# A causal depthwise convolution shared anew between TensorE, VectorE, ScalarE and GpSimd

## The chip, the cores and the metric

The kernel runs on one core of a Trainium2 chip. Its time is the device time of one execution, in microseconds (us). The engines are PE (TensorE, matrix products), DVE (VectorE), ACT (ScalarE), POOL (GpSimd) and SP (SyncE, which issues the DMAs). Each runs its own list of instructions in order and waits for the others through semaphores. SBUF is the working memory of 128 partitions; PSUM holds what PE writes, in eight banks of 128 x 512 float32. POOL works on SBUF only.

## The reference

A trunk of two layers on 256 tokens of width 2048, all in float32. Layer 0 mixes tokens with a convolution module, layer 1 with latent attention; a squared-ReLU MLP follows each. The change touches the convolution module alone:

```python
def conv_module(h, w_pw1, b_pw1, w_dw, b_dw, ln_g, ln_b, w_pw2, b_pw2):
    u = h @ w_pw1 + b_pw1
    a, gate = jnp.split(u, 2, axis=-1)
    u = a * jax.nn.sigmoid(gate)
    u = lax.conv_general_dilated(
        u, w_dw[:, None, :].astype(u.dtype), window_strides=(1,),
        padding=[(CONV_WIDTH - 1, 0)],
        dimension_numbers=("NWC", "WIO", "NWC"),
        feature_group_count=D_MODEL) + b_dw
    u = jax.nn.silu(layer_norm(u, ln_g, ln_b))
    return u @ w_pw2 + b_pw2
```

## The kernel before

Weights come from memory as float32. Each tile of them is split into a rounded part "hi" (by ACT, line 154) and a remainder "lo" (by DVE or POOL, line 155), and a product is made of three fast matmuls: hi with hi, hi with lo, lo with hi. Inputs of the first product, xh and xl, are split the same way once, at the start.

The convolution stage works channel by channel: 16 chunks (KC) of 128 channels, channels on the partitions, 256 tokens along the row. The loop over c from 1 to 16 is software-pipelined by hand, under `tc.manual_schedule()`, so that each engine executes its instructions in the order in which the program writes them. Turn c does the first product of chunk c (`conv_mm`, 96 matmuls, lines 485 to 487, into two PSUM tiles `pss[c]`: values and gates), and the rest of chunk c-1:

- `glu(c-1)`: ACT takes the sigmoid of the gates (line 502), DVE multiplies it with the biased values (line 503). The result `ub` has 30 zeros ahead of it, which POOL writes (line 499). It has three buffers.
- `pe_taps(c-1)`: PE does the first taps. A tap is a product with a diagonal 128 x 128 matrix of its weights (`diag`, made by ACT, line 509), on a window of `ub`. It is a float32 product, which PE runs in two passes (line 518). Chunk 0 has none, chunks 1 to 13 have 3, chunk 14 has 6, chunk 15 has 19. ACT then adds the bias into the same PSUM tile (line 521).
- `dve_taps(c-1)`: DVE does the remaining taps, each one scalar_tensor_tensor (weight times window plus sum, line 552), on a sum in PSUM. It alternates between chunk c-2 and chunk c-1. At the end of a turn 16 taps of chunk c-1 are left over (REST), and a turn begins with four taps of the older chunk (LEAD). Two PSUM banks hold the sums.
- `to_tokens(c-3)`: PE transposes a finished chunk back to tokens (line 579); DVE takes statistics for the layer norm (`ln_stats`, line 589) and ACT copies the tile (line 591).
- `conv_half`: the splits of weight units, four halves in a turn, with lo on POOL.
- From turn 2 on, eight adds on POOL (line 692) put the second product's bias into the residual `xs`.

After the loop come the last chunk's tail (some filler transposes, `keep_warm`, line 220; the last sums, lines 545 and 548), the layer norm (lines 704 to 717), the swish (lines 720 to 737), and the second product with its own loop over m. The chunk's taps, in the order given by these lines, end the stage.

Of the kernel before, what the change touches and what calls it, by code (L numbers as in the profile page):

```python
# [10 lines left out]
F32 = mybir.dt.float32  # L11
# [3 lines left out]
AF = mybir.ActivationFunctionType  # L15
ALU = mybir.AluOpType
AX = mybir.AxisListType

P = 128
D = 2048  # L20
KC = D // P
T = 2
S = T * P
FF = 4 * D
NB = 512
NNB = D // NB
W = 31
PAD = W - 1
# [12 lines left out]
PAD_O = 56  # L41
WB = 6
LOOK = WB // 2 - 1
PE_TAPS = (3, 3, 3, 3)
PE_MORE = (3, 16)
LEAD = 4
REST = (16, 12)
N_WARM = 14
N_WARM_LN = (8, 26, 14)
EPS = 1e-6  # L50
# [22 lines left out]
def trunk_kernel(  # L73
# [26 lines left out]
    nc = tc.nc  # L100
# [8 lines left out]
    def repool(name, **banks):  # L109

        psum_cx[0].close()
        psum_cx[0] = ExitStack()
        for kind, n in banks.items():
            psum[kind] = psum_cx[0].enter_context(tc.tile_pool(name=kind + name, bufs=n, space=PSUM, reuse_waits="tile"))
# [13 lines left out]
    def nm(s):  # L128
        uid[0] += 1
        return f"{s}_{uid[0]}"  # L130


    def acc_tile():
        return psum["acc"].tile([P, NB], F32, tag="acc", name=nm("acc"))

    def tr_tile():
        return psum["tr"].tile([P, NB], F32, tag="tr", name=nm("tr"))
# [107 lines left out]
        for j in range(2):  # L245
            lo_part(ps[j], hi(k0 + j), lo(k0 + j), gain[:, k0 + j : k0 + j + 1])

    repool("c", acc=4, tr=2, sum=2)


    xs = main.tile([P, T, D], F32, name="xs")
# [181 lines left out]
    with ExitStack() as cx:  # L433
# [32 lines left out]
        def conv_half(n, h):  # L466
            if n < NU + KC // 2:
                wjs[n, h] = split_half(raws[n], h, nc.gpsimd if 0 < n + h and n < NU + 2 else nc.vector)
# [17 lines left out]
                    nc.tensor.matmul(o, wh[:, bs], xl(k), start=False, stop=False)  # L486
                    nc.tensor.matmul(o, wl[:, bs], xh(k), start=False, stop=k == KC - 1)  # L487

        pss, ubs, pcs, cas, cts = {}, {}, {}, {}, {}
        n_pe = lambda c: 0 if c == 0 else PE_TAPS[c % 4] + {KC - 2: PE_MORE[0], KC - 1: PE_MORE[1]}.get(c, 0)  # L490
        rest = lambda c: {KC - 2: REST[1], KC - 1: 0}.get(c, REST[0])
        tap = lambda c, w: w_dw[:, w * KC + c : w * KC + c + 1]

        def sum_tile():
            return psum["sum"].tile([P, NB], F32, tag="sum", name=nm("sum"))

        def glu(c):
            ub = ubs[c] = cv2.tile([P, PAD + S], F32, tag="ub", name=nm("ub"), bufs=3)
            nc.gpsimd.memset(ub[:, 0:PAD], 0.0)
            sg = cv2.tile([P, S], F32, tag="sg", name=nm("sg"))  # L500
            va, ga = pss.pop(c)
            nc.scalar.activation(sg, ga[:, :S], AF.Sigmoid, bias=b_pw1[:, KC + c : KC + c + 1])
            nc.vector.scalar_tensor_tensor(
                out=ub[:, PAD:], in0=va[:, :S], scalar=b_pw1[:, c : c + 1], in1=sg, op0=ALU.add, op1=ALU.mult
            )

        def diag(c, w):
            dg = cv2.tile([P, P], F32, tag="dg", name=nm("dg"), bufs=16)
            nc.scalar.activation(dg, ident, AF.Copy, scale=tap(c, w))
            return dg  # L510

        def pe_taps(c, dgs):

            pc = pcs[c] = sum_tile()[:, :S]
            for w in range(n_pe(c)):
                if w == len(dgs):
                    dgs.append(diag(c, w))
                nc.tensor.matmul(pc, dgs[w], ubs[c][:, w : w + S], start=w == 0, stop=w == n_pe(c) - 1)  # L518
            left[c] = list(range(n_pe(c), W))
            if 0 < c < KC - 1:  # L520
                nc.scalar.activation(pc, pc, AF.Identity, bias=b_dw[:, c : c + 1])  # L521
            elif c:

                pcs[c], last_sum[:] = acc_tile()[:, :S], [pc]

        left, last_sum = {}, []

        def ca_part(c):
            if c // 2 not in cas:
                cas[c // 2] = cv2.tile([P, 2, S], F32, tag="ca", name=nm("ca"))  # L530
            return cas[c // 2][:, c % 2, :]

        def dve_tap(c):
            w = left[c].pop(0)
            out = pcs[c]
            if c in (0, KC - 1) and w == n_pe(c):
                nc.vector.tensor_scalar(
                    out, ubs[c][:, w : w + S], scalar1=tap(c, w), scalar2=b_dw[:, c : c + 1],
                    op0=ALU.mult, op1=ALU.add,
                )  # L540
                return
            if c == KC - 1:
                if not left[c]:
                    half = cv2.tile([P, S], F32, tag="half", name=nm("half"), bufs=1)
                    nc.vector.scalar_tensor_tensor(
                        out=half, in0=ubs[c][:, w : w + S], scalar=tap(c, w), in1=out, op0=ALU.mult, op1=ALU.add
                    )
                    nc.vector.tensor_tensor(ca_part(c), last_sum[0], half, op=ALU.add)
                    return
            elif not left[c]:  # L550
                out = ca_part(c)
            nc.vector.scalar_tensor_tensor(  # L552
                out=out, in0=ubs[c][:, w : w + S], scalar=tap(c, w), in1=pcs[c], op0=ALU.mult, op1=ALU.add
            )

        def dve_taps(c, rest, fill):


            n = 0
            while len(left[c]) > rest or left.get(c - 1):  # L560
                if left.get(c - 1):
                    dve_tap(c - 1)
                if n < LEAD and c < KC - 1 and left.get(c - 1):
                    if fill:
                        fill.pop(0)()
                elif len(left[c]) > rest:
                    dve_tap(c)
                n += 1
            while fill:
                fill.pop(0)()  # L570

        def to_tokens(c):

            if c % 2 == 0:
                cts[c // 2] = tr_tile()
            ct = cts[c // 2]
            for t in range(T):
                q = 2 * t + c % 2
                nc.tensor.transpose(
                    ct[:, q * P : (q + 1) * P], cas[c // 2][:, c % 2, t * P : (t + 1) * P], ident  # L580
                )

        def ln_stats(c):
# [22 lines left out]
        with tc.manual_schedule():  # L606
# [27 lines left out]

            def turn0(n):
                for j in range(2):
                    pt = acc_tile() if n == 2 else sum_tile() if n == 1 else None
                    to_T(xn, 4 * n + 2 * j, xh, xl, g_mix[0], pt)


# [18 lines left out]
                turn(w_dw[:, i * NW : (i + 1) * NW], w_rows[i])  # L659
            conv_split(2)  # L660
            conv_mm(0, 12)
            dgs = []
            fills = []
            for c in range(1, KC + 1):
                n = UC * c
                conv_load(n + 3)
                glu(c - 1)
                fills += ln_stats(c - 4) if c > 3 else []
                fill, fills = fills[: 1 + c % 2], fills[1 + c % 2 :]
                if c < KC:  # L670
                    pss[c] = [acc_tile() for _ in range(2)]
                    conv_mm(c, 0, 2)
                conv_half(n + 1, 0)
                pe_taps(c - 1, dgs)
                conv_half(n + 1, 1)
                dve_taps(c - 1, rest(c - 1), fill)
                conv_load(n + 4)
                if c < KC:
                    conv_mm(c, 2, 6)
                    conv_half(n + 2, 0)  # L680
                    conv_half(n + 2, 1)
                    conv_mm(c, 8)
                    dgs = [diag(c, w) for w in range(min(n_pe(c), 16))]
                if c > 2:
                    to_tokens(c - 3)
                if c < KC:
                    conv_mm(c, 12)
                if 2 <= c < 2 + T * NNB:

                    t, i = divmod(c - 2, NNB)  # L690
                    sl = slice(i * NB, (i + 1) * NB)
                    nc.gpsimd.tensor_tensor(xs[:, t, sl], xs[:, t, sl], b2[:, sl], op=ALU.add)
            warm(AF.Sqrt)
            keep_warm(ident, N_WARM_LN[0])
            to_tokens(KC - 2)
            for f in fills + ln_stats(KC - 3):
                f()
            to_tokens(KC - 1)
            for f in ln_stats(KC - 1):
# [47 lines left out]
            for m in range(NP):  # L747
                if m + 3 < NP:
                    ln_norm(m + 3)
                if m + 2 < NP:  # L750
                    ln_swish(m + 2)
                for j in range(2):
                    k = 2 * m + j
                    wh, wl = conv_w(NU + m, j)
                    for b in range(2):
                        bs = slice(b * NB, (b + 1) * NB)
                        for t in range(T):
                            mm3(ps2[b][t], sh_kt(k, t), sl_kt(k, t), wh[:, bs], wl[:, bs], k == 0, k == KC - 1)
                conv_split(NU + m + 2)
                conv_load(NU + m + 5)  # L760

        ssq, add, prepare = residual_stage(True, g_mlp[0])
        for b in range(2):
# [590 lines left out]
```

## Time and profile before

| | |
|---|---|
| time, median of 3 runs | 2014.34 us (2014.23 to 2014.4) |
| the profiled execution | 2014.3 us, span 2012.4 us |
| granted TensorE clock over the span | 0.998 |
| convolution stage | from about 31 us (first sigmoid) to 234.06 us (aggregate of the layer norm's statistics) |

In the profile, a row of a group gives line, engine, operation, output and inputs, shapes, the count, busy time and mean duration in ns, and the idle time ahead of it with what ended it. A row of the timeline begins with its start and duration in us; "x3" means that three neighbours of one kind are merged, and a bracket gives the idle time ahead and its releaser. Instructions of one engine overlap in part: the distance between two starts can be less than a duration.

### The profile page before, as it was taken

To read this page: it belongs to the slowest core of one execution; us is meant where nothing else is said; L and a number is where in the kernel's file an instruction comes from. 1 tells how busy PE (TensorE), PEld (TensorE's weight loads), DVE (VectorE), ACT (ScalarE), POOL (GpSimd) and SP (SyncE) were. 2 spreads that over 40 slices of the span, in tenths; PEclk is the share of its full clock that TensorE was granted. 3 is DMA by queue.
4 is the path that set the end of the run, shared out by engine and by line. 5 is a ranking of instruction groups with operands and counts; after the bars stand their busy time and mean duration, and the time that the engine had idled before them with its cause. 6 is when DMAs were issued, how large, how long until landed. Compare 5 with 4: busy or idle time off the path is not lost.

```text
span 2012.4 us, 28002 instructions
## 1 busy us (share of the span) xinstructions
PE 1989.3 (99%) x11144; PEld 1743.9 (87%) x11144; DVE 1217.5 (61%) x1806; ACT 966.0 (48%) x1372; POOL 209.3 (10%) x156
## 2 busy tenths in 40 slices
PE   7999999999999999999999999999999999999998
PEld 7999888888888888888889998888888888888886
DVE  6999866665554466555546675665654545565453
ACT  5444665544434354444446665544543334454443
POOL 5887300000000000000000510000000000000000
PEclk9999999999999999999999999999999999999999
DMA  7555355666555666555545445666655556665553
GB/s 237 168 168 168 126 188 179 198 189 188 189 197 199 189 189 188 189 192 192 192 144 186 131 146 171 206 190 188 189 192 198 197 188 188 189 189 194 199 192 105
DMA packets 243266, 367.58 MB, mean 183 GB/s; under 512 B 15416, under 2 KB 89792, under 8 KB 242880
## 3 DMA queue, kind: packets, MB, share of 16 engines
q1 hardware_dynamic: 242400, 364.68, 56.9%
q8 instruction: 87, 1.43, 0.3%
q10 hardware_dynamic: 736, 1.12, 0.2%
q14 instruction: 43, 0.35, 0.0%
HBM read 363.68 MB, written 2.10 MB: 182 GB/s over the span
## 4 chain that ended last, share of the span: by engine, by line
PE 96%; DVE 2%; ACT 1%; DMA 0%; issue 0%; POOL 0%; SPq 0%; ACTq 0%; DVEq 0%
PE acc L399 23%; PE acc L182 16%; PE acc L180 16%; PE acc L181 16%; PE acc L400 12%; PE acc L486 3%; PE acc L485 3%; PE acc L487 3%; PE sum L518 1%; PE tr L237 1%; DMA xs<-in_x 0%; PE acc L1128 0%; PE acc L992 0%; PE acc L994 0%; PE acc L993 0%
## 5 line engine op out<-in xcount | busy, mean ns | idle before, releaser
L155 DVE TENSOR_TENSOR lo<-raw,hi 128x1024 fp32r<-128x1024 f32 (+2 forms) x629 | 759.7, 1211 | 694.8 <-ACT hi L154 682.9
L154 ACT ACTIVATE hi<-raw 128x1024 fp32r<-128x1024 f32 (+1 forms) x696 | 723.6, 1046 | 787.3 <-PE acc L181 451.2
L399 PE MATMUL acc<-xt,hi 128*128 128x512 f32 x2048 | 710.6, 390 | 0.0
L400 PE MATMUL acc<-xt,lo 128*128 128x256 f32 x2048 | 577.7, 282 | 0.0
L399 PEld LDWEIGHTS acc<-xt,hi 128*128 128x128 f32 x2048 | 384.4, 188 | 80.5
L180 PE MATMUL acc<-hi,gh 128*128 128x512 f32 x1024 | 398.6, 389 | 0.0
L182 PE MATMUL acc<-lo,gh 128*128 128x512 f32 x1024 | 398.4, 389 | 0.0
L181 PE MATMUL acc<-hi,gl 128*128 128x512 f32 x1024 | 398.4, 389 | 0.0
L400 PEld LDWEIGHTS acc<-xt,lo 128*128 128x128 f32 x2048 | 387.1, 189 | 0.1
L182 PEld LDWEIGHTS acc<-lo,gh 128*128 128x128 f32 x1024 | 192.2, 188 | 39.9
L180 PEld LDWEIGHTS acc<-hi,gh 128*128 128x128 f32 x1024 | 192.2, 188 | 39.8
L181 PEld LDWEIGHTS acc<-hi,gl 128*128 128x128 f32 x1024 | 192.2, 188 | 39.7
L552 DVE SCALAR_TENSOR_TENSOR sum<-ub,w_dw,sum 128x256 f32<-128x256 f32 x404 | 168.5, 483 | 2.8 <-ACT sum L521 0.7
L155 POOL TENSOR_TENSOR lo<-raw,hi 128x1024 fp32r<-128x1024 f32 x67 | 159.3, 2400 | 56.6 <-ACT hi L154 56.6
L485 PE MATMUL acc<-xt,hi 128*128 128x256 f32 x512 | 147.0, 287 | 0.0
L486 PE MATMUL acc<-xt,hi 128*128 128x256 f32 x512 | 143.2, 280 | 1.0 <-DVE xt L193 1.0
L487 PE MATMUL acc<-xt,lo 128*128 128x256 f32 x512 | 143.0, 279 | 0.0
L486 PEld LDWEIGHTS acc<-xt,hi 128*128 128x128 f32 x512 | 96.3, 188 | 1.6 <-DVE xt L193 1.2
L485 PEld LDWEIGHTS acc<-xt,hi 128*128 128x128 f32 x512 | 96.3, 188 | 0.4
L487 PEld LDWEIGHTS acc<-xt,lo 128*128 128x128 f32 x512 | 96.2, 188 | 0.0
L923 POOL MEMSET pad_kv<- 128x8 f32 x1 | 0.1, 105 | 772.6 <-PE acc L182 772.6
L407 ACT ACTIVATE v<-acc 128x256 f32<-128x256 f32 x128 | 46.3, 381 | 25.4 <-PE acc L400 25.4
(230 smaller groups left out, 1787.1 us busy)
## 6 DMA issues: line engine op xcount, KB each, us to landing
raw<-in_mlp_w SPq DMA_DIRECT2D x256, 1024.0 KB, 5.1
raw<-in_conv_w_pw SPq DMA_DIRECT2D x64, 512.0 KB, 5.1
raw<-in_conv_w_pw SPq DMA_DIRECT2D x16, 1024.0 KB, 4.9
raw<-in_mla_w_o SPq DMA_DIRECT2D x16, 1024.0 KB, 5.2
raw<-in_mla_w_kv_up SPq DMA_DIRECT2D x8, 1024.0 KB, 5.4
raw<-in_mla_w_in SPq DMA_DIRECT2D x8, 576.0 KB, 3.7
raw<-in_mla_w_in SPq DMA_DIRECT2D x4, 1024.0 KB, 6.5
raw<-in_mla_w_q_up SPq DMA_DIRECT2D x16, 256.0 KB, 3.6
```

Of the source, the lines that this page charges most:

```text
L154: nc.scalar.activation(hi, raw[:, js, :], AF.Copy)
L155: eng.tensor_tensor(lo, raw[:, js, :], hi.bitcast(F32), op=ALU.subtract)
L180: nc.tensor.matmul(ps, sh, mh, start=start, stop=False)
L181: nc.tensor.matmul(ps, sl, mh, start=False, stop=False)
L182: nc.tensor.matmul(ps, sh, ml, start=False, stop=stop)
L399: nc.tensor.matmul(ps[b], wh[:, bs], xhl(k), start=k == 0, stop=False)
L400: nc.tensor.matmul(ps[b][:, :S], wl[:, bs], xh(k), start=False, stop=k == KC - 1)
L407: nc.scalar.activation(v[:, b, :], o[:, S:], AF.Copy)
L485: nc.tensor.matmul(o, wh[:, bs], xh(k), start=k == 0, stop=False)
L486: nc.tensor.matmul(o, wh[:, bs], xl(k), start=False, stop=False)
L487: nc.tensor.matmul(o, wl[:, bs], xh(k), start=False, stop=k == KC - 1)
L552: nc.vector.scalar_tensor_tensor(out=out, in0=ubs[c][:, w : w + S], scalar=tap(c, w), in1=pcs[c], op0=ALU.mult, op1=ALU.add)
```

## The change

- PE's taps go, but for the last chunk, which has 22 (LAST_PE). Its 22 diagonals are made by ACT over turns 13 to 15.
- For every other chunk, the first tap is done by ACT, bias included, into the PSUM sum (`start_sum`). The next two taps (five in chunk 14, four in chunk 15) are products made by ACT in SBUF (`product`), added to each other by POOL (`side_sum`) and joined to the sum by one DVE add, written as a `None` at position 14 in the chunk's list of taps.
- Gating: ACT copies the values with their bias to SBUF, and POOL multiplies them with the sigmoid. The last chunk is gated by DVE as before.
- DVE's order: a loop takes entries of the two oldest unfinished chunks in turn. The newest chunk begins after 7 entries (LEAD), and a turn ends when 16, 18 and from then on 22 entries of all chunks are left.
- Sums have three PSUM banks, transposes one; some transposes of the start and of the last pair of chunks use other tiles.
- `conv_half(n + 1, 0)` comes ahead of the first product's matmuls, which are no longer cut around the taps.
- The bias adds on `xs` move into the second product's loop.

```diff
-PE_TAPS = (3, 3, 3, 3)
-PE_MORE = (3, 16)
-LEAD = 4
-REST = (16, 12)
+LAST_PE = 22
+SIDE = 2
+LAST_SIDE = (5, 4)
+JOIN = 14
+LEAD = 7
+REST = (16, 18, 22)
...
-    repool("c", acc=4, tr=2, sum=2)
+    repool("c", acc=4, tr=1, sum=3)
...
-            nc.vector.scalar_tensor_tensor(
-                out=ub[:, PAD:], in0=va[:, :S], scalar=b_pw1[:, c : c + 1], in1=sg, op0=ALU.add, op1=ALU.mult
-            )
+            if c == KC - 1:
+
+                nc.vector.scalar_tensor_tensor(
+                    out=ub[:, PAD:], in0=va[:, :S], scalar=b_pw1[:, c : c + 1], in1=sg, op0=ALU.add, op1=ALU.mult
+                )
+            else:
+                vb = cv2.tile([P, S], F32, tag="vb", name=nm("vb"))
+                nc.scalar.activation(vb, va[:, :S], AF.Identity, bias=b_pw1[:, c : c + 1])
+                nc.gpsimd.tensor_tensor(ub[:, PAD:], vb, sg, op=ALU.mult)
+
+        def product(c, w):
+            pr = cv2.tile([P, S], F32, tag="tp", name=nm("tp"), bufs=sum(LAST_SIDE) + SIDE)
+            nc.scalar.activation(pr, ubs[c][:, w : w + S], AF.Copy, scale=tap(c, w))
+            return pr
...
+        def start_sum(c):
+            w = 0
+            if c < KC - 1:
+                pcs[c] = sum_tile()[:, :S]
+                nc.scalar.activation(
+                    pcs[c], ubs[c][:, 0:S], AF.Identity, bias=b_dw[:, c : c + 1], scale=tap(c, 0)
+                )
+                w = 1
+            else:
+                pcs[c] = acc_tile()[:, :S]
+                o = sum_tile()[:, :S]
+                last_sum.append(o)
+                for w in range(LAST_PE):
+                    nc.tensor.matmul(o, dgs[w], ubs[c][:, w : w + S], start=w == 0, stop=w == LAST_PE - 1)
+                w = LAST_PE
+            n = n_side(c)
+            sides[c] = [product(c, w + i) for i in range(n)]
+            left[c] = list(range(w + n, W))
+            left[c].insert(min(JOIN, len(left[c]) - 1), None)
+
+        def side_sum(c):
+            ps = sides[c]
+            step = 1
+            while step < len(ps):
+                for i in range(0, len(ps) - step, 2 * step):
+                    nc.gpsimd.tensor_tensor(ps[i], ps[i], ps[i + step], op=ALU.add)
+                step *= 2
...
         def dve_tap(c):
             w = left[c].pop(0)
             out = pcs[c]
-            if c in (0, KC - 1) and w == n_pe(c):
+            if w is None:
+                nc.vector.tensor_tensor(out, out, sides[c][0], op=ALU.add)
+                return
+            if c == KC - 1 and w == LAST_PE + n_side(c):
...
+        def dve_taps(c, fill):
+
+
+            n, last = 0, turns.get("last")
+            lead = 0 if c in (0, KC - 1) else LEAD
+            while sum(len(v) for v in left.values()) > rest(c):
+                ready = [k for k in sorted(left) if left[k] and (k < c or n >= lead)]
+                if not ready:
+                    break
+                k = next((k for k in ready[:2] if k != last), None)
+                if fill and (k is None or n >= LEAD - 2):
+                    fill.pop(0)()
+                if k is None:
+                    k = ready[0]
+                dve_tap(k)
+                last = turns["last"] = k
                 n += 1
...
-                cts[c // 2] = tr_tile()
+                cts[c // 2] = acc_tile() if c == KC - 2 else tr_tile()
...
-                fills += ln_stats(c - 4) if c > 3 else []
-                fill, fills = fills[: 1 + c % 2], fills[1 + c % 2 :]
+                fill = ln_stats(c - 4) if c > 3 else []
+                fill, copies = fill[:T], fill[T:]
                 if c < KC:
                     pss[c] = [acc_tile() for _ in range(2)]
-                    conv_mm(c, 0, 2)
-                conv_half(n + 1, 0)
-                pe_taps(c - 1, dgs)
+                    conv_half(n + 1, 0)
+                start_sum(c - 1)
+                if c == KC:
+                    side_sum(c - 1)
+                    conv_half(n + 1, 0)
                 conv_half(n + 1, 1)
-                dve_taps(c - 1, rest(c - 1), fill)
+                dve_taps(c - 1, fill)
                 conv_load(n + 4)
                 if c < KC:
-                    conv_mm(c, 2, 6)
+                    side_sum(c - 1)
+                    conv_mm(c, 0, 8)
                     conv_half(n + 2, 0)
                     conv_half(n + 2, 1)
+                    for f in copies:
+                        f()
                     conv_mm(c, 8)
-                    dgs = [diag(c, w) for w in range(min(n_pe(c), 16))]
+                    if c > KC - 4:
+                        dgs.extend(diag(KC - 1, w) for w in range(len(dgs), min(len(dgs) + 8, LAST_PE)))
                 if c > 2:
                     to_tokens(c - 3)
                 if c < KC:
                     conv_mm(c, 12)
-                if 2 <= c < 2 + T * NNB:
-
-                    t, i = divmod(c - 2, NNB)
-                    sl = slice(i * NB, (i + 1) * NB)
-                    nc.gpsimd.tensor_tensor(xs[:, t, sl], xs[:, t, sl], b2[:, sl], op=ALU.add)
...
                 conv_split(NU + m + 2)
                 conv_load(NU + m + 5)
+
+                t, i = divmod(m, NNB)
+                sl = slice(i * NB, (i + 1) * NB)
+                nc.gpsimd.tensor_tensor(xs[:, t, sl], xs[:, t, sl], b2[:, sl], op=ALU.add)
```

## What the time should do: prediction before the run

> **What bounds the kernel now.** The page first: one engine is busy from end to end, and the rows of 40 slices show GpSimd at work in the first six only, which is the convolution stage that the change edits.
>
> ```profile
> span 2012.4 us, 28002 instructions
> PE 1989.3 (99%) x11144; PEld 1743.9 (87%) x11144; DVE 1217.5 (61%) x1806; ACT 966.0 (48%) x1372; POOL 209.3 (10%) x156
> POOL 5887300000000000000000510000000000000000
> 125.00:150.00 25.00, 25.00 (x206) 24.68 (x205) 23.68 (x60) 11.23 (x20) 21.16 (x13) 1.00 0.58 170
> ```
>
> The last row is from the table of stretches (PE, PEld, DVE, ACT, POOL busy, then clock, DMA). The averages over the span mislead: within the stage DVE is 95% busy and POOL 85%, at full clock. I read next the chain of waits there, and the waits of the stage (who for whom: total, times, longest).
>
> ```profile
> 107.16 1.31 PE sum L518 x6
> 119.90 1.31 PE sum L518 x6
> 209.16 2.61 PE sum L518 x12
> ACT sg L502 <- PE acc L487: 85.5, 16, 6.1
> ```
>
> The chain is TensorE's all through: one chunk per 12.74 us (119.90 - 107.16), in which the six passes of three diagonal taps take 1.31. ACT and DVE wait for PE. So PE sets the turn, and DVE stands 5% behind it.
>
> **PE.** Gone are the taps of chunks 1 to 14, 13 x 3 + 6 = 45; a tap is 1.31 / 3 = 0.437. The turn falls to 12.74 - 1.31 = 11.43. The gate inputs give the times:
>
> ```profile
> 31.13 0.47 ACT L502 ACTIVATE sg<-acc,vecs 128x256 f32<-128x256 f32 x1 [4.97 <-PE acc L487]
> 42.33 0.47 ACT L502 ACTIVATE sg<-acc,vecs 128x256 f32<-128x256 f32 x1 [6.06 <-PE acc L487]
> 221.84 0.47 ACT L502 ACTIVATE sg<-acc,vecs 128x256 f32<-128x256 f32 x1 [2.02 <-PE acc L487]
> 27.12 0.38 PE L276 MATMUL tr<-ident,stage 124*128 124x124 f32 x2
> 27.77 0.52 PE L276 MATMUL tr<-ident,stage 124*128 124x124 f32 x2 [0.27 <-DVE w_dw L277]
> ```
>
> A turn without taps and transposes takes 42.33 - 31.13 = 11.20. The transpose pool drops from two banks to one, so the four transposes of the tap weights wait for DVE's copy three times instead of once. One such step is 27.77 - 27.12 = 0.65, against some 0.13 between two that needn't wait (0.38 for a pair): 2 x 0.52 = 1.0 later. Sigmoids then start at 32.1 (chunk 0), 43.3, 54.5, 65.9 (chunk 3), and by PE alone at 65.9 + 12 x 11.43 = 203.1 for chunk 15. It starts at 221.84 today.
>
> **DVE.** It loses the gating STT; a chunk's first tap goes to ACT and two to ACT plus POOL, in place of three on PE, and one add joins them. A turn before: 28 taps, one gating, one bn_stats on average. After: 28 taps, one join, the same bn_stats. The count is equal; only the order differs. Prices:
>
> ```profile
> 227.98 0.39 DVE acc L552
> 228.38 0.39 DVE sum L552
> 32.81 7.32 DVE L552 SCALAR_TENSOR_TENSOR sum<-ub,w_dw,sum 128x256 f32<-128x256 f32 x14
> 107.10 0.42 DVE L589 BATCH_NORM_STATS2 stats<-tr 128x6 f32<-128x256 f32 x1
> 107.44 0.47 DVE L552 SCALAR_TENSOR_TENSOR sum<-ub,w_dw,sum 128x256 f32<-128x256 f32 x1
> 232.39 0.42 DVE L548 TENSOR_TENSOR ca<-sum,half 128x256 f32<-128x256 f32 x1
> ```
>
> Taps that alternate between two sums cost 0.39 each; taps in a row on one sum (14 of chunk 0) cost (7.32 - 0.48) / 13 = 0.53. bn_stats holds DVE for 0.34, and I give the join the same: its nearest row is the add L548 (0.42 long, sources in PSUM and SBUF). Playing the new loop through by hand (7 entries of older chunks, then the two oldest in turn, 22 left over), from turn 5 on no two neighbours share a sum, where today four or two per turn do. An even turn is 28 x 0.39 + 0.34 = 11.3, one with two bn_stats 12.0, mean 11.65. That is above PE's 11.43, so DVE becomes the bound, narrowly. Turn 4 still waits for chunk 3: sigmoid at 65.9, plus bias copy, gating and first tap, 2.25 (below); 22 taps more end at 76.8. Ten turns of 11.65 give 193.3, and turn 15 (27 taps, a join, two bn_stats: 11.6) 204.9. The gating of chunk 15, which stays on DVE, starts there.
>
> **ACT and POOL.** The edits that I cost at nothing are covered as follows.
>
> ```profile
> L502 ACT ACTIVATE sg<-acc,vecs 128x256 f32<-128x256 f32 x16 | 7.6, 476 | 85.5 <-PE acc L487 85.5
> L521 ACT ACTIVATE sum<-sum,vecs 128x256 f32<-128x256 f32 x14 | 6.3, 448 | 19.3 <-PE sum L518 19.3
> L509 ACT ACTIVATE dg<-ident,w_dw 128x128 f32<-128x128 f32 x64 | 20.5, 393 | 0.5 <-PE sum L518 0.4
> L155 POOL TENSOR_TENSOR lo<-raw,hi 128x1024 fp32r<-128x1024 f32 x67 | 159.3, 2400 | 56.6 <-ACT hi L154 56.6
> 110.01 7.12 POOL L155 TENSOR_TENSOR lo<-raw,hi 128x1024 fp32r<-128x1024 f32 x3 [0.32 <-ACT hi L154]
> L692 POOL TENSOR_TENSOR xs<-xs,b 128x512 f32<-128x512 f32 x8 | 10.4, 1302 | 0.0
> L1050 POOL TENSOR_TENSOR qhl<-qp,qhl 128x256 fp32r<-128x256 f32 x8 | 5.9, 746 | 4.1 <-ACT qhl L186 4.1
> ```
>
> ACT drops three diagonals (0.39 each) and gains a bias copy (at most 0.48) and two products (about 0.42); the first tap replaces L521. ACT is 45% busy, so only its order counts. In turns 13 to 15 it adds 22 diagonals, behind all it owes to others. POOL trades one 1.30 add for a gating and a side sum: 128x256 costs 0.75 in another stage (L1050). A turn is four halves at (7.12 - 0.05) / 3 = 2.36, 9.44, plus 1.5, plus a memset of 0.13: 11.05. The gating now waits for ACT, with four splits queued behind it on POOL and the first tap, products and second hi behind it on ACT. From the start of the sigmoid: bias copy to 0.9, gating to 1.65, first split 1.85 to 4.2, next to 6.6, side sum to 7.3, last split ending at 12.0, memset 12.1; the next gating is due at 11.43 + 0.9 = 12.3. PE needs these splits at 5.6, 8.8, 11.4 and 14.2. So POOL fits with 0.2 to spare, and ub plus first tap are ready at 2.25, while DVE has 7 to 11 older entries (2.7 to 4.2) first. Cover gone, all of POOL's excess enters the turn.
>
> Bounds for the two added POOL operations: 0.45 (128x128, L839 below) to 1.30 (twice the width) each; I take 0.75, the same shape.
>
> **The last chunk.**
>
> ```profile
> 222.35 0.48 DVE L503 SCALAR_TENSOR_TENSOR ub<-acc,vecs,sg 128x256 f32<-128x256 f32 x1 [0.35 <-ACT sg L502]
> 222.98 8.44 PE L518 MATMUL sum<-ub,dg 128*128 128x256 f32 x38 [1.18 <-DVE ub L503]
> 234.06 0.58 DVE L704 BATCH_NORM_AGGREGATE mv<-stats 128x2 f32<-128x48 f32 x2
> ```
>
> Today gating to end of L548 is 222.35 to 232.81, 10.45. After, PE's 22 taps run from 204.9 + 0.63 for 44 x 0.2165 + 0.2 = 9.7, to 215.25. DVE has 28 entries; chunk 15's last comes 21st, at about 213, and the final add behind it waits for PE until 215.3. Behind that add stand seven taps of chunk 14, all on one sum: 215.65 + 6 x 0.53 + 0.48 = 219.3. The tail grows to 14.4; the end moves from 232.8 to 219.3, 13.5 earlier, and the aggregate from 234.06 to 220.7 (13.4).
>
> **The moved bias adds.** Eight adds of 1.30 leave POOL's turns. They are written into the second product's loop, yet nothing holds them there: POOL reaches them after the last split, about 213.3, and runs them to 223.3, while DVE passes from aggregate to the first normalised block: 236.58 - 234.06 = 2.5 today, so 220.7 to 223.2. Does POOL hinder DVE? In the attention stage:
>
> ```profile
> 1104.89 0.47 POOL L839 TENSOR_TENSOR m<-scratch,cos 128x128 f32<-128x128 f32 x1
> 1105.31 1.45 POOL L840 TENSOR_TENSOR m<-scratch,sin 128x128 f32<-128x128 f32 x1
> 1104.96 2.89 DVE L155 TENSOR_TENSOR lo<-raw,hi 128x1024 fp32r<-128x1024 f32 x2 [1.68 <-ACT hi L154]
> L155 DVE TENSOR_TENSOR lo<-raw,hi 128x1024 fp32r<-128x1024 f32 (+2 forms) x629 | 759.7, 1211 | 694.8 <-ACT hi L154 682.9
> 236.58 0.88 PE tr L725 x4
> ```
>
> The same POOL operation stretched from 0.47 to 1.45 beside DVE's SBUF-only subtracts, and two of those took 2.89 where two of the mean take 2.42. The taps, with a PSUM source, do not: 67 splits average 2.40. The small operations before the normalisation are SBUF-only. Each may wait out one add; two adds are left by 220.7, so 0 to 2.5. I take 1.2. The Trainium skill (GPSIMD Engine Reference, Specifications) says that the two engines share an SBUF interface and contend when DVE has two SBUF inputs or a 2-port mode; the rows agree, and by the rule the sum would lose the whole 2.5.
>
> Sum: 13.4 - 1.2 = 12.2. The profiled execution took 2014.3 (1.9 beside its span), as the median, 2014.34: forecast 2002.1.
>
> **Rivals.**
> (a) POOL becomes the bound: at 1.30 for each added operation its turn is 9.44 + 0.13 + 2.6 = 12.17. Chunk 15 gates near 65.9 + 12 x 12.17 = 212, the end is 226.4, only 6.4 earlier: 2008. For it: POOL at 85% today; against: 0.75 for this shape.
> (b) Slower: each POOL operation is held up by one DVE tap, as L840 was held. Six operations x 0.48 on 11.05 give 13.9; chunk 15 gates at 233, the end is 247.5: 2029. Against it stand the 67 splits; for it, that gating writes what taps read. Break-even: the gating at 232.8 - 14.4 = 218.4, a turn of 12.7, or 1.55 per added operation.
> (c) PE keeps the pace and the adds collide with nothing: 203.1 + 14.4 = 217.5, 15.3 earlier, 1999.
> (d) The clock drops in the tail. PE idles from its eight filler transposes (end 216.3) to 219.35.
>
> ```profile
> 9.75 3.11 PE L220 MATMUL acc<-ident,xs 128*128 128x128 f32 x14 [0.55 <-DMA xs<-in_x]
> 233.14 3.00 PE L220 MATMUL acc<-ident 128*128 128x128 f32 x26
> ```
>
> After an idle start a filler takes 0.22, later 0.115. Cold, the 26 fillers last 5.8 from 219.9, to 225.7, where the normalised block is due at 223.2: 2.5 later, 2004.6. The Trainium skill (TensorE: Matmul & The Clock Gate, Part 1) puts the drop after an idle window of about 3.4 us; the 3.05 forecast lies just under, so by it the sum stands.
> (e) The change doesn't save: the first tap, two hand-offs late, starves DVE by 12.74 - 11.65 = 1.1 in each turn. Chunk 15 then gates near 65.9 + 12 x 12.74 = 218.8, and the longer tail ends at 233.2, as today: 2014. The first tap would have to come 1.5 later than the 2.25 above.
>
> **How the numbers follow.** Forecast 0.55 (own range 1999.5 to 2004), (a) 0.13, (b) 0.08, (c) 0.13, (d) 0.08, (e) 0.03. The range 1998 to 2009 takes in (a), (c) and (d) and leaves out (b), (e). Faster by over 0.2% (4 us, about what a measurement of this kernel can tell): forecast, (a), (c), (d), 0.89; same 0.03; slower 0.08.
>
> **What would show it.** Right: no L518 group before the last turn; sigmoids 11.4 to 11.7 apart; chunk 15's gating near 205; one DVE wait for PE near 214 with seven taps of one sum behind it; POOL's 128x256 operations at 0.75 and its eight adds under the normalisation. Wrong: DVE waiting each turn for ACT's first tap, POOL's splits above 2.4, PE waiting for lo, or a tail far from 14.4.

## The result and the profile after

The changed kernel takes 2005.29 us (median of 5 runs, 2004.62 to 2007.23) against 2014.34 us: ratio 0.9957, interval 0.9943 to 0.9972. That is 9.05 us less. 2002.1 was forecast, with a range of 1998 to 2009. The profiled execution took 2005.11 us.

First the page: the rows of all engines and of POOL's 40 slices.

```profile
span 2003.3 us, 27860 instructions
PE 1973.8 (99%) x11060; PEld 1730.6 (86%) x11060; DVE 1210.0 (60%) x1797; ACT 975.0 (49%) x1383; POOL 234.7 (12%) x192
POOL 5999400000000000000001410000000000000000
```

PE does 84 passes fewer. POOL is busier over the same stage. The turns are told by the sigmoids (timeline of ACT: chunks 3, 4 and 15), and POOL's prices by its groups:

```profile
66.02 0.47 ACT L509 ACTIVATE sg<-acc,vecs 128x256 f32<-128x256 f32 x1 [5.47 <-PE acc L489]
77.45 0.47 ACT L509 ACTIVATE sg<-acc,vecs 128x256 f32<-128x256 f32 x1 [5.48 <-PE acc L489]
203.14 0.47 ACT L509 ACTIVATE sg<-acc,vecs 128x256 f32<-128x256 f32 x1 [2.04 <-PE acc L489]
...
L518 POOL TENSOR_TENSOR ub<-vb,sg 128x256 f32<-128x256 f32 x15 | 11.1, 743 | 6.5 <-ACT vb L517 6.4
L560 POOL TENSOR_TENSOR tp<-tp,tp 128x256 f32<-128x256 f32 x21 | 15.5, 741 | 1.3 <-ACT tp L522 1.0
L157 POOL TENSOR_TENSOR lo<-raw,hi 128x1024 fp32r<-128x1024 f32 x62 | 147.8, 2407 | 4.9 <-ACT hi L156 3.8 <-issue 1.0
```

A turn takes 77.45 - 66.02 = 11.43, and twelve of them lead to 203.14. The two new POOL operations take 0.74 each, and the splits beside them are as long as before (2.41 for 2.40). So the loop is as forecast. DVE's own turn can be read from its first statistics instruction in turns 5 and 15:

```profile
78.84 0.43 DVE L625 BATCH_NORM_STATS2 stats<-tr 128x6 f32<-128x256 f32 x1
195.16 0.42 DVE L625 BATCH_NORM_STATS2 stats<-tr 128x6 f32<-128x256 f32 x1
203.98 0.48 DVE L512 SCALAR_TENSOR_TENSOR ub<-acc,vecs,sg 128x256 f32<-128x256 f32 x1
```

Ten turns take 116.3: 11.63 each, 0.2 above PE's. The last gating starts at 203.98. It stood at 222.35, so the loop saves 18.4 us, twice what the time shows. The other half is lost behind the loop. The timelines of POOL, PE and DVE from there:

```profile
202.50 4.66 POOL L157 TENSOR_TENSOR lo<-raw,hi 128x1024 fp32r<-128x1024 f32 x2
207.09 0.13 POOL L506 MEMSET ub<- 128x30 f32 x1
215.16 9.85 POOL L799 TENSOR_TENSOR xs<-xs,b 128x512 f32<-128x512 f32 x8
...
207.27 11.29 PE L548 MATMUL sum<-ub,dg 128*128 128x256 f32 x44 [4.17 <-POOL ub L506]
222.71 0.63 PE L615 MATMUL acc<-ident,ca 128*128 128x128 f32 x4 [3.05 <-DVE ca L584]
223.17 4.67 PE L222 MATMUL acc<-ident 128*128 128x128 f32 x26
227.68 1.04 PE L760 MATMUL tr<-ident,cn 128*128 128x128 f32 x8
...
218.60 0.42 DVE L581 TENSOR_TENSOR ca<-sum,half 128x256 f32<-128x256 f32 x1 [5.98 <-PE sum L548]
222.08 0.48 DVE L584 SCALAR_TENSOR_TENSOR ca<-ub,w_dw,sum 128x256 f32<-128x256 f32 x1
224.05 0.58 DVE L739 BATCH_NORM_AGGREGATE mv<-stats 128x2 f32<-128x48 f32 x2
```

PE could begin the last 22 taps at about 204.6, when the gating is done. It waits until 207.27 for the 30 zeros ahead of the last ub, which stand in POOL's queue behind two splits. The taps then take 11.29 instead of the 9.7 expected, DVE waits 5.98 for them, and seven taps of chunk 14 stand behind that wait. In the table of stretches (PE, PEld, DVE, ACT, POOL busy, granted clock, DMA) the clock falls after each idle stretch of PE:

```profile
203.20:207.20 4.00, 0.00 (x0) 0.00 (x0) 4.00 (x12) 0.41 (x1) 4.00 (x3) 0.97 0.16 62
207.20:211.00 3.80, 3.73 (x10) 3.06 (x11) 3.80 (x11) 3.73 (x7) 2.63 (x5) 0.58 0.74 231
219.00:222.60 3.60, 0.65 (x6) 0.41 (x4) 3.39 (x9) 0.00 (x0) 3.60 (x4) 1.00 0.15 63
222.60:226.40 3.80, 3.69 (x24) 3.73 (x25) 3.18 (x13) 2.51 (x4) 2.41 (x2) 0.69 0.00 0
```

The tail from gating to chunk 14's end takes 222.56 - 203.98 = 18.6 us, where 10.45 stood before and 14.4 was forecast. The first transpose of normalised values starts at 227.68, against 236.58 before: 8.9 earlier. That is nearly all of the 9.05, so what follows runs as it did.

### The profile page after: what moved, and what is told of

Its sections match the earlier page's. It is cut to its first block, busy times and chain, and to the rows that moved or that the text cites. A ratio compares the mean times of both kernels' runs of the same rounds, so it can differ in the third digit from the quotient of the medians.

```text
span 2003.3 us, 27860 instructions
## 1 busy us (share of the span) xinstructions
PE 1973.8 (99%) x11060; PEld 1730.6 (86%) x11060; DVE 1210.0 (60%) x1797; ACT 975.0 (49%) x1383; POOL 234.7 (12%) x192
## 4 chain that ended last, share of the span: by engine, by line
PE 96%; ACT 1%; DVE 1%; POOL 1%; issue 0%; DMA 0%; SPq 0%; ACTq 0%; DVEq 0%; POOLq 0%
PE acc L401 23%; PE acc L184 16%; PE acc L183 16%; PE acc L182 16%; PE acc L402 12%; PE acc L488 3%; PE acc L487 3%; PE acc L489 3%; PE tr L239 1%; PE sum L548 1%; DMA xs<-in_x 0%; POOL lo L157 0%; PE acc L1167 0%; ACT hi L156 0%; PE acc L1031 0%
## 5 line engine op out<-in xcount | busy, mean ns | idle before, releaser
L584 DVE SCALAR_TENSOR_TENSOR sum<-ub,w_dw,sum 128x256 f32<-128x256 f32 x402 | 163.8, 484 | 7.5 <-ACT sum L539 6.4
```

Source lines behind the costliest of these rows:

```text
L584: nc.vector.scalar_tensor_tensor(out=out, in0=ubs[c][:, w : w + S], scalar=tap(c, w), in1=pcs[c], op0=ALU.mult, op1=ALU.add)
```

## Experiments

Theory Q: the lost 4 us of the tail are the zeros in POOL's queue and the clock that falls while PE waits for them. Rivals: something that runs beside the taps slows them; the layer norm is late because of POOL's adds, or because of the clock. All edits are to the changed kernel. DVE's and POOL's operations named below are as in the rows above; "gap" is the distance from the start of the aggregate to the start of the first transpose of normalised values, by the rows of the timelines. It was 2.5 before the change and is 3.6 in the changed kernel (the expectation of e2_fill_tail says 3.8, by the chain of waits). The ratio is to the kernel before.

| run | median us | interval of the ratio |
|---|---|---|
| changed kernel | 2005.29 | 0.9943 to 0.9972 |
| e1_zeros | 2002.69 | 0.9928 to 0.9957 |
| e2_fill_tail | 2004.61 | 0.9939 to 0.9968 |
| e3_fill_head | 2004.26 | 0.9936 to 0.9966 |
| e4_add_last | 2003.78 | 0.9932 to 0.9966 |
| e5_zeros_late | 2025.89 | 1.0044 to 1.0071 |
| e6_all | 2023.12 | 1.0031 to 1.0057 |
| e7_gate_dve | 2012.40 | 0.9981 to 0.9999 |
| e8_adds_old | 2011.32 | 0.9979 to 0.9998 |
| e9_zeros_late2 | 2000.61 | 0.9916 to 0.9946 |
| e10_all2 | 1998.24 | 0.9904 to 0.9934 |
| e11_tile | 2029.88 | 1.0060 to 1.0093 |
| e12_tile32 | 2029.74 | 1.0063 to 1.0096 |

**The zeros.**

```diff
-            nc.gpsimd.memset(ub[:, 0:PAD], 0.0)
+            (nc.vector if c == KC - 1 else nc.gpsimd).memset(ub[:, 0:PAD], 0.0)
```

> The 30 zeros ahead of chunk 15's ub are written by DVE just before its gating, not by POOL behind two splits. Theory Q (the queue on POOL delays the last 22 taps, and the wait cools PE's clock): the taps start 0.6 us after the gating's start (now 3.3), PE idles only some 1.4 us, the 44 passes take 9.7 us (now 11.3), the tail from gating to chunk 14's last tap shrinks from 18.6 to 14.4 us, the time from 2005.1 to about 2000.9. Rival R (the passes are slow because POOL's splits or the copies run beside them): the start moves by 2.7, the passes still take 11.3, about 2002.4.

The timelines of PE, DVE and POOL in this run:

```profile
204.77 9.77 PE L548 MATMUL sum<-ub,dg 128*128 128x256 f32 x44 [1.10 <-DVE ub L512]
219.57 3.97 PE L222 MATMUL acc<-ident 128*128 128x128 f32 x26
225.27 1.52 PE L760 MATMUL tr<-ident,cn 128*128 128x128 f32 x8 [1.74 <-DVE cn L750]
...
220.49 0.58 DVE L739 BATCH_NORM_AGGREGATE mv<-stats 128x2 f32<-128x48 f32 x2
221.11 0.82 DVE L204 TENSOR_SCALAR v<-mv 128x2 f32<-128x2 f32 x1
222.20 0.17 DVE L206 RECIPROCAL y<-t 128x2 f32<-128x2 f32 x1 [0.27 <-ACT t L205]
222.40 0.75 DVE L207 TENSOR_TENSOR t<-y 128x2 f32<-128x2 f32 x1
223.18 1.19 DVE L208 TENSOR_TENSOR t<-t,v 128x2 f32<-128x2 f32 x1
...
214.51 9.84 POOL L799 TENSOR_TENSOR xs<-xs,b 128x512 f32<-128x512 f32 x8
```

The taps start 0.5 after the gating and take 9.77: theory Q, against R. The tail is 14.3, as the prediction had it. But 4.2 was expected and 2.6 came. The gap is now 4.8 instead of 2.5: three operations on two columns, 0.16 to 0.2 elsewhere, take 0.75 to 1.19. POOL's adds run from 214.5 to 224.35 here, and the layer norm has moved into them. In the changed kernel it comes 3.6 later, when they are nearly over; only one of these operations is longer there (0.36). That the adds are the cause is argued so far; the runs that hold them back, below, show it.

**Fillers.** Two runs keep PE busy with filler transposes: e2_fill_tail after the taps, e3_fill_head ahead of them.

```diff
-N_WARM_LN = (8, 26, 14)
+N_WARM_LN = (32, 26, 14)        # e2_fill_tail
...
+                if c == KC:
+                    keep_warm(ident, 34)        # e3_fill_head, ahead of start_sum(c - 1)
```

> 32 filler transposes instead of 8 after the taps, so that PE has work in the 3.05 us while DVE ends chunk 14. If the clock drop delays the layer norm: the 26 later fillers take 3.0 us (now 4.67), the first transpose of normalised values comes 2.5 us after the aggregate (now 3.8), the time falls by 1.2 to about 2003.9. If POOL's eight bias adds delay it by holding up DVE: no change, 2005.1.

> 34 filler transposes between the last product and the last 22 taps, with the zeros still written by POOL. If idling cools the clock: taps still start at 207.3 us, but take 9.7 us instead of 11.3, the time falls by 1.6 to about 2003.5. If something beside them slows the passes: no change.

Rows of e2_fill_tail (PE's fillers and first transpose, DVE's aggregate), then PE's taps and fillers in e3_fill_head:

```profile
223.41 3.00 PE L222 MATMUL acc<-ident 128*128 128x128 f32 x26
226.86 1.51 PE L760 MATMUL tr<-ident,cn 128*128 128x128 f32 x8 [0.45 <-DVE cn L750]
224.29 0.58 DVE L739 BATCH_NORM_AGGREGATE mv<-stats 128x2 f32<-128x48 f32 x2
...
207.18 9.77 PE L548 MATMUL sum<-ub,dg 128*128 128x256 f32 x44 [0.48 <-POOL ub L506]
221.98 5.52 PE L222 MATMUL acc<-ident 128*128 128x128 f32 x26
```

e2: the 26 fillers take 3.00 and the gap is 2.57 (224.29 to 226.86). So the clock made the layer norm late in the changed kernel, and not the adds, which cost some 0.2 there. The medians differ by only 0.7 instead of 1.2, and the two sets of runs overlap; the profile decides here. e3: taps start at 207.18 and take 9.77, as expected, with the zeros still late. Of the 1.6 gained at their end, only 0.35 is left at the first transpose (227.33) of the profiled execution: after the later idle stretch the 26 fillers took 5.52 at a clock of 0.50, and the first transpose waited for them. The medians differ by 1.0, and the runs of e3 overlap those of the changed kernel, too.

**PE's add last.**

```diff
-                    nc.vector.tensor_tensor(ca_part(c), last_sum[0], half, op=ALU.add)
+                    turns["half"] = half
...
                 dve_taps(c - 1, fill)
+                if c == KC:
+                    nc.vector.tensor_tensor(ca_part(c - 1), last_sum[0], turns["half"], op=ALU.add)
```

> DVE's add that waits for PE's 22 taps is put behind chunk 14's last seven taps. If those seven taps are on the path: they run in the wait, chunk 14 is done near 216.3, the add follows PE at 218.6, the statistics come 3.5 us earlier, and PE's second idle gap goes too (1.2 more): 2000.4. If only the order counts and the clock still drops: 2001.6. If the seven taps were hidden: no change.

The seven taps ran in the wait, and chunk 14 was done at 216.2 instead of 222.6. PE's second idle stretch vanished, and the 26 fillers took 3.00. But PE's taps took 12.14 in this execution at a clock of 0.50 (0.58 in the changed kernel), so the aggregate came only 2.4 earlier, at 221.68. That again is inside POOL's adds: the gap was 4.3, with the same two operations at 0.74 and 1.19. Result 2003.78, worse than both expectations: a part of this gain goes to the collision with the adds, too.

**POOL's adds held back.** Each of the first five adds is put behind a one-column POOL add (a mark) that reads a normalised block; the other three stand behind these in POOL's queue. e5_zeros_late has this and the zeros on DVE; e6_all has PE's add last as well.

```diff
+                if m + 3 < NP:
+                    last = cn[:, 1, (2 * m + 8) * P - 1 : (2 * m + 8) * P]
+                    mark = small.tile([P, 1], F32, tag="mark", name=nm("mark"))
+                    nc.gpsimd.tensor_tensor(mark, last, last, op=ALU.add)
                 nc.gpsimd.tensor_tensor(xs[:, t, sl], xs[:, t, sl], b2[:, sl], op=ALU.add)
```

> As the run with the zeros on DVE, and each of POOL's bias adds is held back, by a one-column POOL add that reads a normalised block, until the layer norm has passed. If POOL's adds hold up DVE's small operations (three of them took 0.75 to 1.19 us instead of 0.16 to 0.2 in the run with the zeros on DVE alone): all take 0.16 to 0.2 again, aggregate to first transpose shrinks from 4.8 us to 2.5 to 3.1 (the cold fillers then end last), the time falls from 2002.7 to about 2001.0. If the small operations were slow for another reason (the statistics' semaphores, ACT's table load): no change, 2002.7.

> Zeros on DVE, the add that waits for PE behind chunk 14's taps, and the bias adds held back. If the three causes are separate and all of the tail: chunk 14 is done near 216.4, aggregate near 218.3, first transpose near 220.8, no idle gap of PE over 1.5 us, full clock throughout; against 236.58 before that is 15.8 us, so about 1998.5. If the causes overlap: 2000 to 2001.

Both are 25 us slower than expected, though the stage itself did what was expected: all small operations took 0.16 to 0.17, the gaps were 2.5, and the first products of the next stage started at 226.2 and 224.1, against 240.4 before and 231.25 in the changed kernel. The loss is spread over the rest. The groups of e5_zeros_late, and the same of the changed kernel, whose lines 182 to 184 are the three products (hi with hi, hi with lo, lo with hi) of the MLP's second matrices:

```profile
L182 PE MATMUL acc<-hi,gh 128*128 128x512 f32 x1024 | 405.0, 396 | 0.0
L184 PE MATMUL acc<-lo,gh 128*128 128x512 f32 x1024 | 404.8, 395 | 0.0
L183 PE MATMUL acc<-hi,gl 128*128 128x512 f32 x1024 | 404.7, 395 | 0.0
```

```profile
L182 PE MATMUL acc<-hi,gh 128*128 128x512 f32 x1024 | 398.6, 389 | 0.0
L184 PE MATMUL acc<-lo,gh 128*128 128x512 f32 x1024 | 398.4, 389 | 0.0
L183 PE MATMUL acc<-hi,gl 128*128 128x512 f32 x1024 | 398.4, 389 | 0.0
```

Every such product is some 6 ns longer: with those of the two other matrices that line 182 serves (128 each per line), 3 x 1280 = 3840 of them x 6.4 ns = 24.6 us. The only thing in the edit that reaches so far is the new tile for the marks, two buffers of 4 bytes per partition. Theory P: it shifts the tiles behind it. Two runs (e9_zeros_late2 and e10_all2, else as e5 and e6) put the marks into a tile that exists (`tag="warm"`); two others add an unused tile to the changed kernel and nothing else:

```diff
     small.tile([P, PAD_SMALL], F32, tag="pad_small", name="pad_small", bufs=1)
+    small.tile([P, 2], F32, tag="mark", name="mark", bufs=1)        # e11_tile; [P, 8] in e12_tile32
```

> As the run with zeros on DVE and late adds, but the one-column marks go into the tile that ACT's table warm-ups use already, so that no tile of SBUF is added. Theory P (the new 8 bytes per partition shifted the later tiles, and the products of lines 182 to 184 run at 395 ns instead of 389 for it): these are at 389 ns again, aggregate to first transpose 2.5 us, 2000.6. Rival (the late adds or marks slow the rest of the program): 2025 again.

> Zeros on DVE, PE's add last, late adds, marks in the existing tile. The run with all three showed its first product of the second stage 16.5 us earlier than the kernel before (224.12 against 240.66). Theory P: nothing is lost after it, 1997.8. Rival: 2023 again.

> The changed kernel with one more tile of 8 bytes per partition in the pool of small tiles, which nothing reads or writes. Theory P: the products of lines 182 to 184 take 395 ns, some 22 us more, about 2027. Rival: no change, 2005.

> As the run with the unused tile, but of 32 bytes per partition instead of 8. If it is the position of the operands relative to a line of 32 bytes or less that counts: the products take 389 ns again, 2005. If any shift from the tuned layout costs, or a longer line counts: 394 ns or more, over 2020.

A group of e11_tile, whose line 183 is line 182 of the others:

```profile
L183 PE MATMUL acc<-hi,gh 128*128 128x512 f32 x1024 | 405.2, 396 | 0.0
```

Theory P stands: 389 ns and 2000.61 and 1998.24 without a new tile. With 8 unused bytes it is 395 to 396 ns and 24.6 us lost, and with 32 bytes the same. So the first case of e12_tile32's expectation falls: the place in a line of 32 bytes isn't what counts. What does was not tried. The kernel has unused tiles of this kind already (`pad_small` and four others), so its places may have been chosen.

e9 also settles the collision: with the adds held back the three small operations take 0.16 to 0.17, the gap is 2.5, and the time is 2.1 us under that of e1.

Timelines of DVE and PE in e10_all2, the fastest kernel of the study:

```profile
217.84 0.59 DVE L741 BATCH_NORM_AGGREGATE mv<-stats 128x2 f32<-128x48 f32 x2
218.47 0.17 DVE L204 TENSOR_SCALAR v<-mv 128x2 f32<-128x2 f32 x1
...
204.62 9.77 PE L548 MATMUL sum<-ub,dg 128*128 128x256 f32 x44 [1.08 <-DVE ub L512]
216.41 0.68 PE L615 MATMUL acc<-ident,ca 128*128 128x128 f32 x4 [0.93 <-DVE ca L584]
216.93 3.00 PE L222 MATMUL acc<-ident 128*128 128x128 f32 x26
220.37 1.51 PE L762 MATMUL tr<-ident,cn 128*128 128x128 f32 x8 [0.44 <-DVE cn L752]
224.21 0.48 PE L182 MATMUL acc<-hi,sh 128*128 128x512 f32 x1
```

No idle stretch of PE over 1.1 us is left in this stage, nothing is stretched, and the four runs lie within 0.4 us where those of the changed kernel spread over 2.6. It beats the changed kernel by 7.05 and the kernel before by 16.2 us; its first product of the next stage starts 16.2 earlier (224.21 against 240.42).

**How near the other engines are.** Gating back on DVE for all chunks, and the bias adds back in POOL's turns 2 to 9:

```diff
-            if c == KC - 1:
+            if True:        # e7_gate_dve, in glu(c): always the branch on nc.vector
```

> Gating of all chunks on DVE, as before; the rest of the change stays. If DVE is the next bound, close behind PE: its turn grows by 0.39 to about 12.0, the last gating comes at about 208.3 us instead of 204.0, the last 22 taps start about 208.9, 1.6 later than now, since POOL's zeros then come first: about 2006.5. If PE alone sets the pace and DVE has room: the last gating stays near 204, and the time does not change or falls a little as POOL's queue is shorter.

The same eight adds as before the change, at the end of turn c (e8_adds_old):

```diff
+                if 2 <= c < 2 + T * NNB:
+                    t, i = divmod(c - 2, NNB)
+                    sl = slice(i * NB, (i + 1) * NB)
+                    nc.gpsimd.tensor_tensor(xs[:, t, sl], xs[:, t, sl], b2[:, sl], op=ALU.add)
```

> The eight bias adds stay in POOL's turns 2 to 9, where they were before; the rest of the change stays. POOL's turn is then 11.05 + 1.25 = 12.3 us in those turns. If POOL has only 0.2 us of room per turn: it falls back by about 0.85 per turn, the splits reach PE late after two or three turns, the last gating comes 4 to 6 us later, and the time is 2009 to 2011, though the layer norm is free of the adds. If POOL has room: 2005 or less.

The sigmoids in e7_gate_dve (chunks 8, 10) and in e8_adds_old (chunks 5, 6):

```profile
123.60 0.47 ACT L509 ACTIVATE sg<-acc,vecs 128x256 f32<-128x256 f32 x1 [3.56 <-PE acc L489]
147.64 0.47 ACT L509 ACTIVATE sg<-acc,vecs 128x256 f32<-128x256 f32 x1 [3.55 <-PE acc L489]
```

```profile
90.46 0.47 ACT L509 ACTIVATE sg<-acc,vecs 128x256 f32<-128x256 f32 x1 [3.55 <-PE acc L489]
102.84 0.47 ACT L509 ACTIVATE sg<-acc,vecs 128x256 f32<-128x256 f32 x1 [4.05 <-PE acc L489]
```

With one more operation DVE's turn is (147.64 - 123.60) / 2 = 12.02, and with one more add POOL's is 12.3 to 12.4. So DVE's turn without the gating stands 0.2 above PE's 11.43, and POOL's without the add of 1.25 some 0.3 below it, about as priced. e8 has the time expected, just above its upper end. e7 does not (2012.40 for 2006.5): its last gating came at 210.23 instead of 208.3, and the zeros did not come first. POOL, whose splits wait for an ACT that waits for DVE's gating (24.9 us in all), wrote them at 213.26, 4.4 after the last sigmoid, so the taps started at 213.45 instead of 208.9.

## Why the prediction was right, and where not

- **PE's turn, the start with one transpose bank.** 11.43 each and a first sigmoid at 32.19 (32.1 forecast); chunk 15's at 203.14 (203.1).
- **DVE's turn.** 11.63 measured, 11.65 forecast. The last gating came at 203.98, 0.9 earlier than the 204.9 forecast: turn 15 has 25 taps, a join and two bn_stats, where the sum had 27 taps; two taps are 0.8.
- **POOL and ACT in the loop.** Gating and side sum 0.74 each for 0.75; the turn fits, with about the room that the sum gave it (e8). Rivals (a), (b) and (e) fell: no operation of POOL was stretched in the loop, and DVE never waited for a first tap after turn 4. Rival (c) was right about the adds, nearly, but not about the pace: DVE's turn is above PE's.
- **The last chunk: the step that failed.** The sum put PE's taps 0.63 behind the gating, for a clock at full speed. It looked at the last gating, which stays on DVE, and not at the zeros that share its tile and stay on POOL, behind two splits and a side sum of four adds. They cost 2.66 of waiting, and 1.5 more through the clock, which I had not allowed for in this gap (e1 and e3 separate the two). Together 4.2: with them 14.4 becomes the 18.6 measured, and with the 0.9 above taken off, 2002.1 becomes 2005.4. With the zeros moved, the tail is 14.3 and the time 2002.69.
- **The add that waits for PE and the seven taps behind it.** As forecast: they stand behind the wait, 3.96 from the add's start to chunk 14's end, and are worth moving.
- **The moved bias adds.** 1.2 was taken of 0 to 2.5. The mechanism is right: 2.3 in e1, where the layer norm comes when the forecast had it, and nothing in e9, where the adds are held back. That the bound held has some luck in it: POOL began its adds at 214.51 there instead of 213.3, so three were left and not two. In the changed kernel the later tail steps out of their way, and they cost 0.2. One row was misread on the way: the mean of 1.21 for DVE's subtracts mixes three shapes, and those of 128x1024 alone have 1.23, so two take 2.46 where the prediction has 2.42; the 2.89 is still longer.
- **Rival (d), the clock in the tail.** Forecast: an idle stretch of 3.05, price 2.5, chance 0.08. The stretch was 3.05, and the clock did fall: 0.69 in the next stretch, the fillers took 4.67, and the gap was 3.6 instead of 2.5. So 1.1 was lost there, 0.2 of it by the adds and the rest by the fillers, where the sum had 1.2 for the adds. That the two sizes agree is luck, and e2 shows it. The Trainium skill (TensorE: Matmul & The Clock Gate, Part 1) has the drop after an idle window of some 3.4 us, by which the sum was to stand; the trace disagrees for this stretch. After the same idle stretch of 3.05 to 3.06 the fillers ran slow in the changed kernel, e1, e3 and e11, and at full speed in e5, e7, e8, e9 and e12. PE's instructions up to there are the same in e1, e5 and e9, so the program does not decide it. The page also calls the window free-running. That would let the outcome differ from one execution to the next, as it does, but no stretch of 3.05 holds a whole window of 3.4, so what sets it stays open here. The longer stretch ahead of the taps, 4.16 to 4.62, was followed by slow taps in all seven runs that have it (11.29 to 12.20 for 9.77).

## What to carry to other kernels

When work is moved between engines, follow every small instruction that the moved or kept work still needs, down to a memset of 30 columns: its queue has changed too, and it can hold up the engine on the critical path for as long as whatever stands ahead of it. An operation that was moved to where it seems free runs as early as its queue lets it, not where the program is written; look at which time it falls into, and what runs beside it there. Before any edit that adds a tile, however small, compare the mean duration of the great groups of matmuls before and after, since a shift of tiles can cost more than the edit earns.

## What was not expected of the hardware

- 8 or 32 unused bytes per partition, in one more tile, made the 128x512 products of lines 182 to 184 last 395 to 396 ns instead of 389, and the program 24.6 and 24.5 us longer. The products of lines 401 and 402 (390 and 282 ns) did not change. Which operand's place counts was not tried.
- Some DVE operations on two columns, with SBUF operands alone, last up to 1.19 instead of 0.16 while POOL works through adds of 1.27 each. Each of the three stretched ones in e1 ends within 0.03 us of one of the adds (224.37 and 224.35 for the last). The reciprocal among them, also on two columns, took its 0.17. The Trainium skill (GPSIMD Engine Reference, Specifications) names the shared interface; the size of the wait, about the rest of the add in flight, is from these runs.
